# Where the last weights of a two-layer decoder wait, and in which order its first tiles are asked for

## The chip, the cores and the metric

The kernel runs on one core of one Trainium2 chip, in one launch. The metric is device time in microseconds (us), the median of several runs. Everything below comes from those times and from one profiled execution of the kernel before.

## What is computed

Two layers of a hybrid decoder over 1104 tokens (1024 of a prompt, 16 learned ones ahead of it, 64 of eight sampled sequences), width 1024, float32. Cut to what matters:

```python
def trunk_layer(x, pos, lw, states, front_pad, chunk, attend):
    m, new_states = hybrid_mixer(rmsnorm(x, lw['g_pre_mix']), pos, lw, states, front_pad, chunk, attend)
    x = x + rmsnorm(m, lw['g_post_mix'])
    gate, up = jnp.split(rmsnorm(x, lw['g_pre_ffn']) @ lw['w_ffn_in'], 2, axis=-1)
    x = x + rmsnorm((jax.nn.silu(gate) * up) @ lw['w_ffn_out'], lw['g_post_ffn'])
    return x, new_states
```

The mixer projects the normalized input (`w_in`), runs three token mixers on its columns (gated delta rule, a state space model, sliding-window attention with rotary positions) and projects back (`w_out`). The hidden width of the last block (SwiGLU) is 2816.

## The kernel before

**Arithmetic.** Each float32 operand of a large matrix product is split into two float16 parts, a rounded one (an ACT cast) and a residual (a VectorE operation), and a product takes three matmuls: high by high, high by low, low by high. For a weight this split is made on the chip, piece by piece: a piece of 128 x 1024 is loaded raw, cast, and its residual taken.

**Tiles.** Tokens stand in nine tiles of 128 (the last has 80), so `NT` is 9. The last projection of a layer (`w_ffn_out`) is done in seven half-size products, in Strassen's manner, instead of eight: `FSEQ` (line 35) gives their order 1, 2, 5, 6, 3, 7, 4. Their weights are blocks of `w_ffn_out` or sums and differences of blocks. Products 7 and 4, the last two, take a difference between a raw block and a running sum that is kept in `tcx`. Each product walks over 11 blocks of rows in six pieces (the last piece is half as long), and has four output tiles of 128 tokens, plus a fifth of 80 in four of the seven.

**Order.** There is no order written out by hand. `Plan` (from line 116) keeps a clock for each engine from rough costs, and `run` takes generators by rank: the first in rank order whose inputs are due by TensorE's planned time goes on by one step, and if none is due, the one due first. Small ranks come first: 0 for norms and chains, 2 for the sums of the hidden activations (`hid_sums`), 3 for the two `loader` generators, 9 for `dense`, which issues the large products. The framework beneath may then move an instruction ahead on its engine when its own simulation has it ready sooner; DMA issues on SP are moved in this way too.

**Slots.** `big` hands out 23 general slots (`NG`), counted by `live`: `hold` takes one, `free` gives one back, `room(n)` waits for n. Beside them stand two raw slots (`rawp`, counted in `wfree["raw"]`), three slots `w`, and three slots `w2` in the last block. The queue that `order_loads` fills sets the order of all weight loads: `loader` takes the next piece when a raw slot is free, issues its DMA, waits until it is that piece's turn to be split and until it has somewhere to go (`avail`), splits it, and gives the raw slot back. For products 7 and 4 the queue alternates between a piece of 7 and one of 4. Pieces of 7 go to `w2`; of product 4 the first five go to general slots, the last to `w2`. `dense` drops a piece when all output tiles of its group are done; the groups of a product are pieces 0, 1, 2, 3 and then 4 with 5.

**Norms.** `ffn_post` runs after the last projection, in two generators of rank 0: per tile it loads the residual stream, squares and sums on ACT, takes the reciprocal root on POOL (`rsqrt`), multiplies by the gain and adds on VectorE, and stores. In layer 0 it goes on with the norm that makes layer 1's input (`norm_t`): another square, POOL step and product, eight transposes on TensorE, and casts and residuals. It starts for four tiles after product 3, and for the other four after product 4.

**Start.** `norm0` loads and norms the tiles of x; `first_load` loads and splits the four pieces of the first weight. Four `norm0` generators are started among the first loads, so four tiles of x are asked for early, and each later one when a generator has finished a tile.

Of the kernel before, what the change touches and what calls it, by code (L numbers as in the profile page):

```python
# [8 lines left out]
F32 = mybir.dt.float32  # L9
# [30 lines left out]
def tsz(i):  # L40
    return 128 if i < 8 else 80
# [74 lines left out]
class Plan:  # L116
# [9 lines left out]
    def __init__(self):  # L126
        self.clk = dict.fromkeys("TVSGD", 0.0)
        self.wr = {}
        self.done = {}
        self.banks, self.start, self.acc = {}, {}, {}  # L130
        self.tasks = []
        self.last = 0.0

# [72 lines left out]
    def engine(self, eng, k):  # L206
        plan = self

        class E:
            def __getattr__(self, name):  # L210
                f = getattr(eng, name)

                def call(*a, **kw):
                    r = f(*a, **kw)  # L214
                    aps = [x for x in list(a) + [v for n, v in kw.items() if n not in ("out", "accum_out")]
                           if isinstance(x, bass.AP)]
                    out = kw.get("out")
                    if out is None:
                        out, aps = aps[0], aps[1:]
                    plan.note(k, name, out, aps, [kw["accum_out"]] if "accum_out" in kw else [],  # L220
                              kw.get("op") is ALU.pow)
                    return r

                return call

        return E()
# [55 lines left out]
def build(tc, A, depth=DEPTH):  # L282
    nc = tc.nc
    P = Plan()
    V, S, G, T, DQ = (P.engine(e, k) for e, k in ((nc.vector, "V"), (nc.scalar, "S"), (nc.gpsimd, "G"),
# [176 lines left out]
    def loader():  # L462
        while True:
            yield lambda: wfree["raw"] > 0 and took[0] < len(queue) and not seven[0]
            if wfree["raw"] == 0 or took[0] == len(queue) or seven[0]:
                continue
# [6 lines left out]
            if src is not None:  # L473
                wfree["raw"] -= 1
                raw = rawp.tile([128, 1024], F32, tag="raw", name="raw")[:, :n]
                dma(raw, src)
# [5 lines left out]
            def avail():  # L482
                if split[0] != my:
                    return False
                if where == "t":
                    return key[2] == 0 or ("ffn", key[1]) in done and (
                        wfree["w2"] > 0 if key[2] != 4 or key[3] == 5 else live[0] < NG)
# [14 lines left out]
            if where == "f":  # L502
                where = "w2" if wfree["w2"] else "w"
            elif where == "t":
                where = "g" if key[2] == 4 and key[3] < 5 else "w2"
            elif where != "w":
                where = "g"
# [18 lines left out]
            if src is not None:  # L526
                wfree["raw"] += 1
# [160 lines left out]
    def order_loads(L):  # L688
# [16 lines left out]
        for ns in ((1,), (2, 0), (5,), (6,), (3,), (7, 4)):  # L705
# [125 lines left out]
    def dense():  # L831
        for L in LY[:depth]:
# [234 lines left out]
            for n in FSEQ:  # L1067
                bk = [psd.tile([128, 512], F32, tag="d", name="pd") for _ in range(2)] + [PS("o") for _ in range(2)]
                for g in ((0,), (1,), (2,), (3,), (4, 5)):
# [63 lines left out]
    def norm0(L, it):  # L1133
        for i in it:
            C = tsz(i)
            yield room(1)
            hold()
            xt = big([128, D], F32, "xt")
            dma(xt[:C], A["x"][i * 128:i * 128 + C, :])
            yield None  # L1140
            yield (("gb0",),)
# [974 lines left out]
    P.add(0, norm0(L, it))  # L2116
    P.run()
    dma(c32, A["c32"])
    load_g(0, 0, L.gb0)
    for s in range(4):  # L2120
        P.add(-1, first_load(s))
        P.run()
        if s in (1, 2):
            P.add(0, norm0(L, it))
            P.run()
    P.add(0, norm0(L, it))
    P.add(3, loader())
    P.add(3, loader())
    P.add(0, when([("xn", 0, i) for i in range(NT)], free))
    mark(("gb0",))  # L2130
    P.add(9, dense())
    P.add(1, setup(L))
    for L in LY[:depth]:
# [10 lines left out]
        P.run(("swaend", l), ("gates", l), *((("zt", l, i), "st") for i in range(NT)))  # L2144
        sub.close()
# [40 lines left out]
        P.add(0, ffn_post(L, it))  # L2186
        P.add(0, ffn_post(L, it))
# [92 lines left out]
```

## Time and profile before

| | us |
|---|---|
| median of 3 runs | 2901.14 |
| lowest and highest | 2896.04 and 2902.44 |
| the profiled execution | 2895.58 |
| its span, first to last instruction | 2893.5 |
| TensorE busy / VectorE busy / ACT busy / POOL busy | 2743.2 / 1933.3 / 1288.4 / 813.1 |
| mean granted TensorE clock | 0.981 |

The profile names an instruction by its engine (PE is TensorE, PEld its weight loads, DVE is VectorE, POOL is GpSimd, SP issues the DMAs), by what it writes and reads (`wsp<-raw` is a split of a raw piece, `hsp<-hid` one of the hidden activations, `rqy<-ss` the reciprocal root of a norm, `m` and `xt` the output and the residual stream of a tile), and by its shape. All lines are line 214, the recorder through which every call goes. An idle time stands in brackets with what ended it. A busy share tells how full an engine is; TensorE's own time also depends on its granted clock, of which 1.0 is 2.4 GHz and 0.5 is 1.2 GHz.

### The profile page before, as it was taken

What the parts mean: (1) busy time and instruction counts of PE and PEld (TensorE: products, weight loads), DVE (VectorE), ACT (ScalarE), POOL (GpSimd) and SP (SyncE); (2) the same over time, 40 slices, a digit from 0 to 9 for tenths busy, and PEclk for the clock granted to TensorE, in tenths of its full rate; (3) what the DMA queues carried; (4) which work ended last, traced back from release to release, by engine and by line L of the source; (5) the groups of instructions that cost most, each with busy time, mean ns of one, the idle gap of its engine ahead of it and who ended that gap; (6) DMA issues with size and microseconds to landing.
All of it is one profiled execution on the core that took longest, in us unless ns stands there. A gap on an engine that the chain in (4) does not pass through costs nothing. (4 is left out here: it accounts for less than half of the span.)

```text
span 2893.5 us, 50019 instructions
## 1 busy us (share of the span) xinstructions
PE 2743.2 (95%) x19662; PEld 1909.5 (66%) x19662; DVE 1933.3 (67%) x3614; ACT 1288.4 (45%) x3015; POOL 813.1 (28%) x1124
## 2 busy tenths in 40 slices
PE   6999999999799999999899999999998999999997
PEld 3766677664588888744348676777646888886443
DVE  5557667655757676767865676666457666766776
ACT  5435456554423333433544455655543333334342
POOL 2204523313543333200260062223136233231011
PEclk8999999999899999999999999999999999999998
DMA  5011110132301111242431111001222111113333
GB/s 183 31 60 37 57 38 31 38 104 89 109 30 59 53 51 59 96 120 68 163 128 34 50 47 46 31 31 56 86 103 87 50 54 59 52 52 110 106 115 124
DMA packets 74092, 209.79 MB, mean 73 GB/s; under 512 B 13360, under 2 KB 24816, under 8 KB 73824
## 3 DMA queue, kind: packets, MB, share of 16 engines
q1 hardware_dynamic: 73856, 206.59, 21.8%
q8 instruction: 154, 2.52, 0.4%
q14 instruction: 82, 0.67, 0.1%
HBM read 175.49 MB, written 33.04 MB: 72 GB/s over the span
## 5 line engine op out<-in xcount | busy, mean ns | idle before, releaser
L214 PEld LDWEIGHTS <-wsp 128*128 128x128 f16 x10704 | 1044.1, 99 | 305.7 <-issue 12.9
L214 PE MATMUL pd<-xn,wsp 128*128 128x336 f16 (+3 forms) x4512 | 737.7, 311 | 3.4 <-DVE a L214 3.1
L214 DVE SCALAR_TENSOR_TENSOR wsp<-raw,wsp 128x512 f16<-128x512 f32 (+2 forms) x414 | 404.8, 986 | 196.3 <-ACT wsp L214 193.5
L214 ACT ACTIVATE wsp<-raw 128x512 f16<-128x512 f32 (+2 forms) x414 | 311.0, 763 | 393.5 <-DVE raw L214 145.9
L214 PEld LDWEIGHTS <-hsp 128*128 128x128 f16 x1848 | 182.1, 99 | 242.0 <-issue 30.2
L214 PE MATMUL pd<-wsp,hsp 128*128 128x512 f16 x924 | 232.6, 385 | 17.1 <-ACT wsp L214 11.8
L214 PE MATMUL ps_o<-wsp,hsp 128*128 128x512 f16 x924 | 230.7, 383 | 0.5 <-DVE m L214 0.5
L214 PE MATMUL pd<-wsp,mixed 128*128 128x512 f16 (+1 forms) x864 | 212.0, 384 | 5.8 <-DVE m L214 5.8
L214 POOL TENSOR_SCALAR rqy<-ss 128x1 f32<-128x1 f32 (+1 forms) x72 | 56.1, 779 | 551.1 <-ACT jk L214 407.6
L214 DVE SCALAR_TENSOR_TENSOR u<-R,lp_cw,u 128x512 f32<-128x512 f32 x216 | 180.0, 869 | 4.3 <-ACT u L214 3.4
L214 ACT ACTIVATE hsp<-hid 128x512 f16<-128x512 f32 x154 | 89.8, 620 | 180.4 <-PE ps_o L214 143.7
L214 PE MATMUL pd<-wsp,xn 128*128 128x512 f16 (+3 forms) x864 | 161.2, 338 | 6.0 <-ACT wsp L214 3.4
L214 PE MATMUL ps_o<-xn,wsp 128*128 128x256 f16 (+1 forms) x1296 | 165.1, 285 | 0.0
L214 POOL TENSOR_TENSOR raw<-raw 128x512 f32<-128x512 f32 x74 | 95.5, 1292 | 241.9 <-DVE raw L214 208.4
L214 PE MATMUL ps_inv<-xn,wsp 128*128 128x256 f16 (+1 forms) x1248 | 154.0, 281 | 0.8 <-DVE a L214 0.8
L214 POOL TENSOR_TENSOR U<-U,hid 128x256 f32<-128x256 f32 (+1 forms) x114 | 80.3, 733 | 239.3 <-ACT hid L214 239.3
L214 PEld LDWEIGHTS <-mixed 128*128 128x128 f16 (+1 forms) x864 | 84.4, 101 | 82.4 <-issue 11.3
L214 DVE TENSOR_TENSOR hsp<-hid,hsp 128x512 f16<-128x512 f32 x154 | 101.4, 684 | 43.3 <-ACT hsp L214 43.3
L214 PEld LDWEIGHTS <-xn 128*128 128x128 f16 (+1 forms) x864 | 87.4, 103 | 55.9 <-issue 10.7
L214 PE MATMUL ps_ch<-xn,wsp 128*128 128x296 f16 x456 | 109.2, 289 | 0.0
L214 PE MATMUL ps_tr<-xn,wsp 128*128 128x256 f16 x456 | 108.6, 273 | 0.0
L214 DVE TENSOR_TENSOR W<-ps_inv,c 128x512 f16<-128x512 f32 (+1 forms) x120 | 71.0, 595 | 46.3 <-PE ps_inv L214 45.4
(496 smaller groups left out, 4738.9 us busy)
## 6 DMA issues: line engine op xcount, KB each, us to landing
raw<-wfi SPq DMA_DIRECT2D x88, 512.0 KB, 3.5
raw<-wfo SPq DMA_DIRECT2D x70, 512.0 KB, 3.7
raw<-wf SPq DMA_DIRECT2D x44, 512.0 KB, 3.3
xd<-xt SPq DMA_DIRECT2D x24, 512.0 KB, 2.9
xt<-xd SPq DMA_DIRECT2D x24, 512.0 KB, 5.7
xt<-x SPq DMA_DIRECT2D x16, 512.0 KB, 6.1
raw<-wo SPq DMA_DIRECT2D x16, 512.0 KB, 3.4
tcx<-wfo SPq DMA_DIRECT2D x10, 512.0 KB, 3.7
```

Source lines behind the costliest of these rows:

```text
L214: r = f(*a, **kw)
```

## The change

Five things. Raw pieces of products 7 and 4 no longer use the two raw slots: each takes a general slot (tag `rawg`), which it gives back after its split; a loader may start on them even when no raw slot is free. All pieces of 7 now come ahead of those of 4 in the queue, all finished pieces of 4 go to `w2`, and product 4's last group is made of pieces 3, 4 and 5. There are three loaders instead of two. The two `ffn_post` generators have rank 4 instead of 0, behind `hid_sums` (2) and the loaders (3). At the start `load_x` asks for all nine tiles of x by itself: the first ahead of the constants, one more with each of the later pieces of the first weight, and the rest at once behind the fourth; three `norm0` generators then only compute. And until the attention of layer 0 has ended, every DMA issue is pinned behind the one before it on SP (`P.pin`), so that the framework no longer moves them.

```diff
--- before.py
+++ after.py
@@ -130,6 +130,7 @@
         self.banks, self.start, self.acc = {}, {}, {}
         self.tasks = []
         self.last = 0.0
+        self.pin = None
 
     @staticmethod
     def box(a):
@@ -212,6 +213,8 @@
 
                 def call(*a, **kw):
                     r = f(*a, **kw)
+                    if k == "D" and plan.pin is not None:
+                        plan.pin(r)
                     aps = [x for x in list(a) + [v for n, v in kw.items() if n not in ("out", "accum_out")]
                            if isinstance(x, bass.AP)]
                     out = kw.get("out")
@@ -282,6 +285,7 @@
 def build(tc, A, depth=DEPTH):
     nc = tc.nc
     P = Plan()
+    P.pin = tc.keep_in_program_order
     V, S, G, T, DQ = (P.engine(e, k) for e, k in ((nc.vector, "V"), (nc.scalar, "S"), (nc.gpsimd, "G"),
                                                  (nc.tensor, "T"), (nc.sync, "D")))
     dma = DQ.dma_start
@@ -461,8 +465,11 @@
 
     def loader():
         while True:
-            yield lambda: wfree["raw"] > 0 and took[0] < len(queue) and not seven[0]
-            if wfree["raw"] == 0 or took[0] == len(queue) or seven[0]:
+            def more():
+                k = took[0] < len(queue) and queue[took[0]][0]
+                return k and (wfree["raw"] > 0 or k[0] == "w2" and k[2] in (7, 4)) and not seven[0]
+            yield more
+            if not more():
                 continue
             my = took[0]
             took[0] += 1
@@ -470,7 +477,13 @@
             if where == "s":
                 yield from load7(my, key, src)
                 continue
-            if src is not None:
+            spare = key[0] == "w2" and key[2] in (7, 4)
+            if spare:
+                yield room(1)
+                hold()
+                raw = big([128, 1024], F32, "rawg")[:, :n]
+                dma(raw, src)
+            elif src is not None:
                 wfree["raw"] -= 1
                 raw = rawp.tile([128, 1024], F32, tag="raw", name="raw")[:, :n]
                 dma(raw, src)
@@ -483,8 +496,7 @@
                 if split[0] != my:
                     return False
                 if where == "t":
-                    return key[2] == 0 or ("ffn", key[1]) in done and (
-                        wfree["w2"] > 0 if key[2] != 4 or key[3] == 5 else live[0] < NG)
+                    return key[2] == 0 or ("ffn", key[1]) in done and wfree["w2"] > 0
                 if where == "f":
                     return ("ffn", key[1]) in done and wfree["w2"] + wfree["w"] > 0
                 if where == "w":
@@ -502,7 +514,7 @@
             if where == "f":
                 where = "w2" if wfree["w2"] else "w"
             elif where == "t":
-                where = "g" if key[2] == 4 and key[3] < 5 else "w2"
+                where = "w2"
             elif where != "w":
                 where = "g"
             if where == "g":
@@ -523,7 +535,9 @@
             stt(w[:, 1, :n], x, WS, w[:, 0, :n], MUL, SUB)
             if key[0] == "w2" and key[2] == 5:
                 V.tensor_tensor(x, raw, x, op=SUB)
-            if src is not None:
+            if spare:
+                free()
+            elif src is not None:
                 wfree["raw"] += 1
             if key[0] == "w2" and key[2:] == (4, 5):
                 mark(("tcend", key[1]))
@@ -702,7 +716,7 @@
                     want(("wi", l, c, z), src[z], 1024, "f")
             else:
                 want(("wi", l, c), src, 1024, "s")
-        for ns in ((1,), (2, 0), (5,), (6,), (3,), (7, 4)):
+        for ns in ((1,), (2, 0), (5,), (6,), (3,), (7,), (4,)):
             for n, s in [x for s in range(7) for x in ((ns[0], s), (ns[-1], s - 1))[:len(ns)] if 0 <= x[1] < 6]:
                 want(("w2", l, n, s), None if n == 6 else wfo(l, *FW[n], s), (2 if s < 5 else 1) * 512, "t")
 
@@ -1066,7 +1080,7 @@
                    for i in range(8)}
             for n in FSEQ:
                 bk = [psd.tile([128, 512], F32, tag="d", name="pd") for _ in range(2)] + [PS("o") for _ in range(2)]
-                for g in ((0,), (1,), (2,), (3,), (4, 5)):
+                for g in ((0,), (1,), (2,), (3,), (4, 5)) if n != 4 else ((0,), (1,), (2,), (3, 4, 5)):
                     yield tuple((x, l, n, q) for x in ("w2", "S2") for q in g)
                     ks = range(2 * g[0], min(2 * g[-1] + 2, NF // 2))
                     for t in (0, 2, 1, 3, 4):
@@ -1132,13 +1146,7 @@
 
     def norm0(L, it):
         for i in it:
-            C = tsz(i)
-            yield room(1)
-            hold()
-            xt = big([128, D], F32, "xt")
-            dma(xt[:C], A["x"][i * 128:i * 128 + C, :])
-            yield None
-            yield (("gb0",),)
+            xt, C = L.x0[i], tsz(i)
             yield from norm_t(xt, C, i, L.gb0, L.xn, xt, "n")
             free()
             mark(("xn", 0, i))
@@ -2113,21 +2121,27 @@
     L = LY[0]
     it = iter(range(NT))
     L.gb0 = big([128, D], F32, "gb0")
-    P.add(0, norm0(L, it))
-    P.run()
+    L.x0 = []
+
+    def load_x(n):
+        for i in range(len(L.x0), n):
+            hold()
+            L.x0.append(big([128, D], F32, "xt"))
+            dma(L.x0[i][:tsz(i)], A["x"][i * 128:i * 128 + tsz(i), :])
+
+    load_x(1)
     dma(c32, A["c32"])
     load_g(0, 0, L.gb0)
-    for s in range(4):
+    for s, n in enumerate((1, 2, 3, 4)):
         P.add(-1, first_load(s))
         P.run()
-        if s in (1, 2):
-            P.add(0, norm0(L, it))
-            P.run()
-    P.add(0, norm0(L, it))
-    P.add(3, loader())
-    P.add(3, loader())
+        load_x(n)
+    load_x(NT)
+    for _ in range(3):
+        P.add(0, norm0(L, it))
+    for _ in range(3):
+        P.add(3, loader())
     P.add(0, when([("xn", 0, i) for i in range(NT)], free))
-    mark(("gb0",))
     P.add(9, dense())
     P.add(1, setup(L))
     for L in LY[:depth]:
@@ -2142,6 +2156,7 @@
         P.add(0, swa_out(L))
         P.add(1, gates(L))
         P.run(("swaend", l), ("gates", l), *((("zt", l, i), "st") for i in range(NT)))
+        P.pin = None
         sub.close()
         sub = ExitStack()
         L.ssp = pool("ssm", 1, stack=sub)
@@ -2183,8 +2198,8 @@
         if not L.last:
             P.add(1, setup(LY[l + 1]))
         it = iter((0, 1, 2, 3, 8, 4, 5, 6, 7))
-        P.add(0, ffn_post(L, it))
-        P.add(0, ffn_post(L, it))
+        P.add(4, ffn_post(L, it))
+        P.add(4, ffn_post(L, it))
         P.run(("dense", l), *(x for i in range(NT) for x in (("fp", l, i), (("x", l, i), "st"))))
         wfree["w2"] = 0
         free(2 if L.last else 3)
```

## Rows read from the trace of the kernel before

**Rows 1.** Page, part 1: busy us, share of the span, instructions.

```profile
PE 2743.2 (95%) x19662; PEld 1909.5 (66%) x19662; DVE 1933.3 (67%) x3614; ACT 1288.4 (45%) x3015; POOL 813.1 (28%) x1124
```

**Rows 2.** Windows: length, busy us (instructions) by engine, PE clock, DMA share, GB/s.

```profile
0.00:75.00 75.00, 48.79 (x249) 27.85 (x249) 37.45 (x66) 37.01 (x85) 23.17 (x45) 0.86 0.52 177
...
1385.00:1463.00 78.00, 67.68 (x310) 30.53 (x309) 69.81 (x83) 41.34 (x67) 17.58 (x19) 0.96 0.54 177
1463.00:1500.00 37.00, 31.98 (x161) 16.15 (x160) 26.11 (x41) 17.49 (x34) 27.56 (x35) 0.95 0.36 110
2810.00:2882.00 72.00, 62.60 (x268) 27.06 (x266) 53.61 (x64) 26.08 (x40) 13.78 (x10) 0.93 0.39 129
2882.00:2894.00 12.00, 0.23 (x2) 0.00 (x0) 7.81 (x8) 2.30 (x4) 3.57 (x5) 0.70 0.43 175
```

**Rows 3.** Windows of 25 us: the same point of layer 0 and layer 1.

```profile
300.00:325.00 25.00, 20.54 (x150) 15.19 (x150) 22.14 (x48) 11.67 (x35) 14.52 (x19) 0.97 0.15 47
...
1725.00:1750.00 25.00, 20.52 (x144) 14.93 (x143) 20.81 (x45) 10.33 (x31) 14.05 (x19) 0.93 0.14 42
```

**Rows 4.** Timeline of layer 1's product 7: start, length, engine, operation, count.

```profile
2810.63 1.46 PE L214 MATMUL pd<-wsp,hsp 128*128 128x512 f16 x6
...
2811.93 1.46 PE L214 MATMUL ps_o<-wsp,hsp 128*128 128x512 f16 x6
```

**Rows 5.** Timeline of the start; in brackets idle time and what ended it.

```profile
8.48 1.11 PE L214 MATMUL ps_tr<-c,xt 128*128 128x128 f32 x4 [8.48 <-DVE xt L214]
...
14.53 0.43 SPq L214 DMA_DIRECT2D raw<-wtA  x1
...
17.85 8.13 SPq L214 DMA_DIRECT2D xt<-x  x5
...
23.37 1.06 ACT L214 ACTIVATE wsp<-raw 128x1024 f16<-128x1024 f32 x1
...
45.12 1.06 ACT L214 ACTIVATE xn<-xt 80x1024 f16<-80x1024 f32 x1 [1.05 <-POOL rqy L214]
```

**Rows 6.** Windows of 5 us, columns as in rows 2.

```profile
10.00:15.00 5.00, 4.56 (x15) 1.34 (x14) 3.19 (x5) 1.91 (x3) 0.00 (x0) 1.00 1.09 287
35.00:40.00 5.00, 4.71 (x15) 2.58 (x15) 1.89 (x2) 3.92 (x9) 4.63 (x7) 0.50 0.28 110
2815.00:2820.00 5.00, 5.00 (x25) 2.29 (x24) 5.00 (x6) 2.16 (x5) 5.00 (x1) 1.00 0.59 166
```

**Rows 7.** Groups by shape, 1385 to 1463 us: busy us, mean ns | idle before.

```profile
L214 DVE SCALAR_TENSOR_TENSOR m<-xt,rqy,gb 128x1024 f32<-128x1024 f32 x4 | 5.1, 1279 | 1.3 <-POOL rqy L214 1.3
...
L214 PE MATMUL ps_tr<-c,m 128*128 128x128 f32 x16 | 2.5, 282 | 1.4 <-DVE m L214 1.4
```

**Rows 8.** Groups by shape, 2810 to 2882 us, columns as in rows 7.

```profile
L214 DVE TENSOR_TENSOR hsp<-hid,hsp 128x512 f16<-128x512 f32 x20 | 13.3, 684 | 7.8 <-ACT hsp L214 7.8
...
L214 DVE SCALAR_TENSOR_TENSOR wsp<-raw,wsp 128x1024 f16<-128x1024 f32 x9 | 11.0, 1221 | 1.6 <-ACT wsp L214 1.6
...
L214 ACT ACTIVATE wsp<-raw 128x1024 f16<-128x1024 f32 x8 | 8.4, 1053 | 12.8 <-DVE raw L214 12.8
...
L214 DVE SCALAR_TENSOR_TENSOR xt<-m,rqy,xt 128x1024 f32<-128x1024 f32 x5 | 6.4, 1279 | 0.8 <-POOL rqy L214 0.7
...
L214 DVE TENSOR_TENSOR raw<-raw,tcx 128x1024 f32<-128x1024 f32 x4 | 4.9, 1216 | 0.0
```

**Rows 9.** Timeline of products 7 and 4 in layer 1.

```profile
2815.86 3.21 SPq L214 DMA_DIRECT2D raw<-wfo  x2
...
2826.52 0.59 PE L214 MATMUL pd<-wsp,hsp 128*128 128x512 f16 x1 [5.37 <-ACT wsp L214]
...
2842.17 0.38 PE L214 MATMUL pd<-wsp,hsp 128*128 128x512 f16 x1 [2.24 <-ACT wsp L214]
```

**Rows 10.** Timeline of the end.

```profile
2887.34 2.47 DVE L214 SCALAR_TENSOR_TENSOR xt<-m,rqy,xt 128x1024 f32<-128x1024 f32 x2
```

**Rows 11.** POOL's norm step, 2800 us to the end: ns least/median/most, first and last start.

```profile
L214 POOL TENSOR_SCALAR rqy<-ss x9: 190/1221/7667, 2805.6 to 2885.3; 128x1 f32<-128x1 f32 x8, 80x1 f32<-80x1 f32 x1
```

## The prediction, written before the result was known

> **What bounds the kernel now.** I read the page's busy times first: TensorE is busy 2743.2 us, 95% of the span, VectorE 1933.3 [rows 1]. So TensorE sets the end, and time can be won only where it is idle or at its lower clock. Next comes the busy time by stage: nearly every window is full of TensorE; three places are not, and the change touches all three [rows 2]. The start: 48.79 us busy of the first 75.00, granted clock 0.86. The seam between the layers (last products of layer 0, then the first projection of layer 1): 10.3 us idle of 78.00, then 5.0 of 37.00. The last products of layer 1: 9.4 us idle of 72.00 at clock 0.93, and after the last matmul (0.23 us into the last window, so at 2882.23) 11 us with no TensorE.
>
> How much the start loses is read by comparing the layers. The window 300 to 325 us has 20.54 us of TensorE, the window 1725 to 1750 has 20.52 [rows 3]: the same point of the layer. Layer 0 comes to it 300 us after the span's start; layer 1 comes to it 262 us after 1463, where its first projection begins (the cut of rows 2). So the start costs 38 us more than a start with everything at hand.
>
> For the last two products (7 and 4) I need their floor. Six matmuls start at 2810.63 and the next six at 2811.93 [rows 4], so one takes 0.216 us; the two products have 2 x 11 x 4 x 3 = 264 of them: 57.0 us. In layer 1 they take 72, so 15.0 are lost: 9.4 idle, and clock 0.93 means 14% of 72, about 10 us, at the 1.2 GHz level, where half the progress is lost: 5.0. The sum, 14.4, agrees.
>
> **The change, part by part. Start.** Nothing is removed; transfers are moved. Before, the fourth piece of the first weight was asked for at 14.53 us, behind constants, the next weight and copies of caches; five tiles of x followed from 17.85, and that issue took 8.13 us, each waiting for earlier transfers [rows 5]. Now SP's queue keeps program order: x0, constants, gain, four weight pieces with x1 to x3 between, then x4 to x8. Up to the fourth piece and x3 that is, by their shapes, 0.52 MB x 9 + 0.3 = 5.0 MB. At the 287 GB/s of the window 10 to 15 us [rows 6] this needs 17 us, and some 2 more to land: the fourth piece is there at 17 to 19 us and all of x (2.4 MB more) by 27, where before the fourth split ran at 23.37 and the square of the last tile at 45.12 [rows 5]. TensorE still cannot start before 8.48 [rows 5], and to finish the first tile it needs the fourth piece. A tile costs it 24 x 0.216 = 5.2 and eight transposes at 2.5 / 16 each [rows 7], together 6.4 us, more than VectorE's 2.7 for its norm (1.28 + 2 x 0.68 [rows 7, 8]), so once x is there TensorE sets the pace. Loss after, as an estimate: 12 idle (18 less one tile's 6.4), up to 4 before the second tile, 3 at the low clock, 6 for waits inside the attention steps, together 25 against 38. I take **-12**; bounds -3 (the tiles were late by engine queues, not by transfers) and -17 (no gap and almost no waits). What is moved behind x (rotary tables, second weight, cache copies, convolution weights: some 4 MB, 14 us) lands near 41 us. SP's pinned order could hold a load behind a store that waits for its engine; the cover is that from 75 us on TensorE works from weights already split. If it is gone, a first rotary step waits a few us on POOL, while TensorE has nine tiles of projection to do: 0, bound +3.
>
> **Last products, layer 1.** Before, two raw slots alternate between a piece of 7 and one of 4, and a slot comes back only after VectorE's residual, which stands behind norm work. So the third piece of 7 is asked for at 2815.86, and TensorE stops 5.37 us at 2826.52, then 2.24 at 2842.17 [rows 9]. The change gives each raw piece a general slot, has three in flight, takes all of 7 ahead of 4, and lets splits go before norms. Number and duration of the splits stay: 1.22 for the difference, 1.22 for the residual, 0.68 for each half-width operation [rows 8]. VectorE's whole work in the window is 53.61 us [rows 2], below the 57.0 floor, so it has room if the order is right. What the change takes away: product 4 loses its five general slots for finished weights and shares three with product 7. Such a slot comes free two groups (10.4 us) before its next piece is needed; difference, cast and residual need 1.22 + 1.05 + 1.22 = 3.5 [rows 8]. Its last group, of three pieces, needs the last of them right after the second group, but twelve matmuls (2.6 us) come ahead of it. For this and for the change from 7 to 4 I leave 4 of the 14.4: **-10.5**; bounds -14 and -4.
>
> **Tail.** The last group of product 4 has five blocks instead of three, so its four output tiles finish 15 x 0.216 = 3.24 us apart, not 1.94. One tile's eviction, gain and addition need 0.68 + 1.22 + 1.28 = 3.2 us of VectorE [rows 8], so no queue builds up. Today two additions run until 2889.8 [rows 10], 7.6 us after the last matmul; one tile's chain without a queue (0.68, then 1.05, POOL's two steps, 1.28 and the hops) ends about 5 us after it. **-2.5**; bounds -4 and 0 (five norms now rank lower and may land here, but the last 13 us of matmuls ask little else of VectorE).
>
> **Seam.** Here norms also make layer 1's input, so a tile costs VectorE 1.22 + 1.28 + 1.28 + 2 x 0.68 = 5.1 us [rows 7, 8]. In the 115 us of both windows VectorE is busy 95.9 and TensorE 99.7 [rows 2], the latter about 95 at full clock. So no more than 19 us can be had, and VectorE becomes the bound as soon as TensorE's waits go. Splits put first push norms into the projection; that alone does not lose, since a tile costs TensorE 6.4 there against 5.1. With VectorE nine tenths busy the 115 become 106.6: I take **-7**; bounds -14 and 0.
>
> Elsewhere the third loader finds no raw slot, except where a piece needs none: 0, bounds 3 either way, since the planner's order shifts.
>
> Sum: -12 - 10.5 - 2.5 - 7 = -32. The profiled execution took 2895.6 us in all (its span 2893.5); 2895.6 - 32 = 2863.6. The median of the runs shown, 2901.1, is 5.5 higher, and I carry that over: **2869**.
>
> **A rule against it.** POOL's small step of a norm takes 0.19 us at best in the last stretch and 7.67 at worst [rows 11]; in the window 2815 to 2820, inside that worst one, POOL holds one instruction for 5.00 us while VectorE is busy 5.00 of 5.00 [rows 6]. The Trainium skill ("SBUF — State Buffer", section "Who interferes with whom") has VectorE with two SBUF inputs and GpSimd reading SBUF exclude each other, the later one blocking fully. By that rule, with which the row agrees, splits packed ahead of norms keep POOL out longer.
>
> **The rivals.** First, x was not the limit: the last tile's load was issued by 26 us, its square ran at 45.12 [rows 5]. Against it: transfers still moved 110 GB/s at 35 to 40 us [rows 6]. Then the start gives 3, not 12: 2878. Second, the ranking does nothing, because the planner takes a norm when it comes ready and a split only when VectorE is due to be free; only the earlier loads work, and half of the products' and the seam's gain stays away: 2869 + 5 + 3.5, about 2878. Third, norms starve: POOL's step finds no gap, as in its 7.67 us, the gains and additions of five tiles (5 x 2.5 = 12.5 us) run after the last matmul, and the seam gives nothing: 2869 + 12.5 + 7, about 2888. Against it stands VectorE's room in the last group. Fourth, slower: product 4 with three slots waits at each piece. It decides when more than 10.4 - 3.5 = 6.9 us of other VectorE work stands ahead of a split; two norms of layer 0 make 10.2, so it can. Each wait costs what the second of layer 1 did, 2.24 idle and about 1.9 of low clock; five pieces in two layers make 41 us. Against these stand the start's 12, the tail's 2.5 and product 7's first wait (5.4 and 3 of clock in layer 1, perhaps 5 in layer 0): +13, so 2914. Fifth, the change doesn't do what it says: engine orders replace each wait by another: 2901.
>
> **How the numbers follow.** Forecast 0.55; rivals one to five 0.12, 0.10, 0.10, 0.08, 0.05. The first three are faster too, by more than 0.2% (5.8 us, about what a measurement of this kernel can tell from no change). So faster 0.87, same 0.05, slower 0.08. The range: down to 2869 - 17 = 2852, where each part comes near its better bound; up to 2889, which takes in the first three rivals. Left out are the last two rivals (0.13) and about 0.07 beside.
>
> **What the profile would show.** Start: the fourth piece split before 20 us, the last tile's square before 32, TensorE busy over 58 of the first 75 us; the step is wrong under 52. Products in layer 1: about 61 us for 7 and 4 and no wait above 2 us inside 7; wrong if a wait for a cast or residual stands at each piece of 4. Seam: VectorE over nine tenths busy until the last norm; wrong if the projection still waits for norms. Tail: under 9.5 us from the last matmul to the end. The whole is wrong if the stage 75 to 1385 us, which I leave alone, moves by more than 3 us.

## The result, and where the time went

| | us |
|---|---|
| kernel after, median of 4 runs | 2858.06 (2854.41 to 2860.39) |
| kernel before, beside it, median of 4 runs | 2898.91 (2896.04 to 2902.44) |
| ratio, with its 95% interval | 0.9857 (0.9839 to 0.9875) |
| profiled execution after, its span | 2859.83, 2858.0 |

The change saves 40.85 us, 1.4%. The two profiled executions differ by 35.5 us in span; the other 5 are the choice of execution: that of before lies just below the runs shown, that of after near the top of its own.

Both kernels run the same stages in the same order, so the span can be cut where a stage's first matmul starts or a store begins:

| stage (us) | before | after | difference | forecast |
|---|---|---|---|---|
| start, to the store of layer 0's convolution states | 588.8 | 577.5 | -11.3 | -12 |
| from there to layer 0's product 7 | 796.9 | 798.4 | +1.5 | 0 |
| layer 0, products 7 and 4 | 77.2 | 69.5 | -7.7 | seam: |
| first stage of layer 1, to its store | 549.6 | 544.9 | -4.7 | -7 together |
| from there to layer 1's product 7 | 798.1 | 798.4 | +0.3 | 0 |
| layer 1, products 7 and 4 | 71.6 | 58.9 | -12.7 | -10.5 |
| last matmul to the end | 11.3 | 10.4 | -0.9 | -2.5 |
| sum | 2893.5 | 2858.0 | -35.5 | -32 |

Page of after, part 1 (busy us, share of the span, instructions), and windows of after that answer to [rows 1, 2] (length, busy us (instructions) by engine, PE clock, DMA share, GB/s):

```profile
PE 2730.1 (96%) x19662; PEld 1907.6 (67%) x19662; DVE 1938.0 (68%) x3614; ACT 1287.5 (45%) x3015; POOL 820.8 (29%) x1124
```

```profile
0.00:75.00 75.00, 56.42 (x326) 34.32 (x327) 49.02 (x83) 43.80 (x103) 28.18 (x50) 0.91 0.56 185
...
1376.00:1445.50 69.50, 63.42 (x291) 29.56 (x290) 61.88 (x74) 37.27 (x59) 23.71 (x20) 0.95 0.44 140
1445.50:1482.50 37.00, 37.00 (x198) 19.65 (x197) 26.86 (x35) 15.63 (x30) 31.20 (x38) 1.00 0.36 118
2788.70:2847.60 58.90, 57.44 (x265) 25.54 (x263) 51.41 (x62) 25.11 (x38) 14.98 (x9) 1.00 0.45 145
2847.60:2858.00 10.40, 0.00 (x0) 0.00 (x0) 6.07 (x6) 1.65 (x4) 3.56 (x4) 0.68 0.38 151
```

The recorder's line is 215 now, for 214. The number of instructions on each of these engines is as before, and VectorE's time is 4.7 us above it. TensorE's busy time falls by 13.1 us with the same matmuls (its mean granted clock rises from 0.981 to 0.984), its idle time by 22.4. Layer 1's products are now full but for 1.46 us, at granted clock 1.00, where 0.93 stood. In layer 1's first projection TensorE is busy 37.00 of 37.00, where it was 31.98, while VectorE has only 26.86: it is not what bounds there.

The waits of TensorE inside layer 1's products (engine and tile that waited, for whom: us in total, times, longest) have one line left, where [rows 9] showed waits of 5.37 and 2.24 for casts:

```profile
PE pd L215 <- DVE hsp L215: 1.5, 1, 1.5
```

SP's timeline of the start and ACT's, which answer to [rows 5] (start, length, operation):

```profile
2.58 0.44 SPq L215 DMA_DIRECT2D lp_cw<-cw  x1
...
4.01 0.45 SPq L215 DMA_DIRECT2D raw<-wtB  x1
4.50 0.43 SPq L215 DMA_DIRECT2D raw<-wtA  x1
...
8.79 0.43 SPq L215 DMA_DIRECT2D xt<-x  x1
9.27 0.43 SPq L215 DMA_DIRECT2D raw<-wtA  x1
...
10.21 0.84 SPq L215 DMA_DIRECT2D k_s<-ck  x1
...
11.53 0.43 SPq L215 DMA_DIRECT2D raw<-wtA  x1
12.01 0.68 SPq L215 DMA_DIRECT2D v_s<-cv  x1
12.74 6.29 SPq L215 DMA_DIRECT2D xt<-x  x6
```

```profile
20.29 1.04 ACT L215 ACTIVATE wsp<-raw 128x1024 f16<-128x1024 f32 x1
...
36.13 1.05 ACT L215 ACTIVATE xn<-xt 80x1024 f16<-80x1024 f32 x1
```

The pin does not do what the diff seems to say. Convolution constants, pieces of the second weight and copies of caches still stand ahead of x1 and of the later weight pieces. In program order the constants come behind x8. Read from the program, the pin hangs each DMA on the last instruction traced on SP, whatever that is, and ahead of the constants that is not x8's DMA, so from there the chain floats as a whole; no run shows this reason by itself. What is traced after `P.pin = None` (layer 1's constants, for one) is not held at all. Still, the last six tiles of x are asked for from 12.74 us, where it was five from 17.85, and the fourth weight piece at 11.53 instead of 14.53.

### The profile page after: what moved, and what is told of

Its sections match the earlier page's. It is cut to its first block, busy times and chain, and to the rows that moved or that the text cites. A ratio compares the mean times of both kernels' runs of the same rounds, so it can differ in the third digit from the quotient of the medians.

```text
span 2858.0 us, 50012 instructions
## 1 busy us (share of the span) xinstructions
PE 2730.1 (96%) x19662; PEld 1907.6 (67%) x19662; DVE 1938.0 (68%) x3614; ACT 1287.5 (45%) x3015; POOL 820.8 (29%) x1124
## 5 line engine op out<-in xcount | busy, mean ns | idle before, releaser
L215 PEld LDWEIGHTS <-wsp 128*128 128x128 f16 x10704 | 1044.4, 99 | 306.3 <-issue 14.6
L215 DVE SCALAR_TENSOR_TENSOR wsp<-raw,wsp 128x512 f16<-128x512 f32 (+2 forms) x390 | 377.4, 977 | 184.1 <-ACT wsp L215 181.3
L215 ACT ACTIVATE wsp<-raw 128x512 f16<-128x512 f32 (+2 forms) x390 | 287.4, 749 | 367.3 <-DVE raw L215 106.5
L215 PE MATMUL pd<-wsp,hsp 128*128 128x512 f16 x924 | 224.5, 381 | 3.8 <-DVE hsp L215 1.9
L215 PE MATMUL ps_o<-wsp,hsp 128*128 128x512 f16 x924 | 222.5, 379 | 0.0
L215 POOL TENSOR_SCALAR rqy<-ss 128x1 f32<-128x1 f32 (+1 forms) x72 | 65.5, 910 | 528.1 <-ACT jk L215 390.9
L215 DVE SCALAR_TENSOR_TENSOR u<-R,lp_cw,u 128x512 f32<-128x512 f32 x216 | 180.3, 870 | 11.3 <-ACT u L215 10.3
```

## The experiments

All are edits of the kernel after. The table gives the stages as above, and the ratio to the kernel before, measured beside each. The first two rows are the kernels before and after. Stages are in us, each from one profiled execution.

| kernel | start | L0 7+4 | L1 first | L1 7+4 | tail | median us | ratio (95%) |
|---|---|---|---|---|---|---|---|
| before | 588.8 | 77.2 | 549.6 | 71.6 | 11.3 | 2898.9 | |
| after | 577.5 | 69.5 | 544.9 | 58.9 | 10.4 | 2858.1 | 0.9857 (0.9839 to 0.9875) |
| after again | 577.1 | 68.1 | 545.2 | 59.0 | 10.4 | 2856.0 | 0.9846 (0.9827 to 0.9866) |
| start alone | 575.1 | 77.6 | 552.9 | 70.8 | 11.6 | 2883.3 | 0.9954 (0.9941 to 0.9966) |
| last products alone | 591.2 | 68.1 | 548.1 | 58.9 | 10.4 | 2873.1 | 0.9911 (0.9897 to 0.9924) |
| no pin | 578.6 | 67.9 | 544.9 | 58.9 | 10.4 | 2863.1 | 0.9879 (0.9865 to 0.9892) |
| pin that holds | 575.6 | 68.2 | 547.9 | 58.9 | 10.5 | 2859.3 | 0.9867 (0.9851 to 0.9882) |
| norms at rank 0 | 574.7 | 68.6 | 551.3 | 58.9 | 10.4 | 2861.5 | 0.9867 (0.9852 to 0.9882) |
| two loaders | 574.8 | 68.0 | 548.8 | 58.8 | 10.5 | 2857.8 | 0.9853 (0.9836 to 0.9869) |
| raw slots | 572.9 | 66.8 | 558.0 | 64.6 | 9.7 | 2871.5 | 0.9904 (0.9889 to 0.9918) |
| small last group | 576.6 | 71.4 | 561.8 | 59.0 | 11.6 | 2877.1 | 0.9921 (0.9906 to 0.9936) |
| small group, layer 1 | 574.8 | 68.4 | 544.7 | 58.9 | 11.2 | 2857.2 | 0.9852 (0.9838 to 0.9867) |
| three norm generators | 575.1 | 66.9 | 553.4 | 59.6 | 10.5 | 2865.0 | 0.9888 (0.9872 to 0.9905) |
| the same, pin that holds | 575.5 | 67.0 | 554.2 | 59.6 | 10.5 | 2866.7 | 0.9891 (0.9876 to 0.9906) |

### The unchanged kernel again

> The kernel after once more, unchanged: how far do the stages of one program differ between two executions? Six kernels with the same start had the store of layer 0's convolution states at 572.9 to 577.5. Theory (that spread comes from the planned order, which each edit shifts): here it is at 577.5 within 0.3, and layer 1's first stage (end of product 4 to that layer's store) is 544.9 within 0.5. Rival (it is the execution): the first differs by 1 to 3, the second by over 1.

The store stands at 577.1, the first stage of layer 1 takes 545.2, each within 0.4 us of the first execution (products 7 and 4 of layer 0 differ by 1.4). Two executions say little about a spread, but other kernels below say more. Up to the store, the traces of eight more executions (this one, start alone, norms at rank 0, two loaders, raw slots, both kernels with small groups, three norm generators) hold the same operations on the same tiles in the same order as after's, on every engine. Their stores begin at 572.9 to 577.1, with after's nine executions from 572.9 to 577.5, 575.4 on the mean. So that spread is not the planned order, as the theory had it: the order is one, and the execution makes the difference. In the same way last products alone, no pin, pin that holds and small group in layer 1 have after's order between the two stores: their first stage of layer 1 takes 544.7 to 548.1 us, and layer 0's products 7 and 4 take 67.9 to 69.5. In the start a difference of less than 5 us, and in that stage one of less than 3.5, is not put down to a kernel here.

Inside the start this execution was later: the fourth piece split at 22.50 us, the last tile's square at 38.16, 2 us behind the first execution. Still at 249 us, after's TensorE was 4.0 us ahead (its 1600th matmul at 249.1, here at 253.1). It lost most of that with TensorE as busy but at a lower granted clock, as the windows of after and of this execution show:

```profile
300.00:400.00 100.00, 96.33 (x736) 68.29 (x735) 60.24 (x120) 50.28 (x116) 22.95 (x40) 0.95 0.13 44
```

```profile
300.00:400.00 100.00, 96.29 (x749) 69.09 (x747) 61.61 (x127) 51.40 (x118) 22.90 (x41) 0.97 0.13 44
```

Between 200 and 300 us the clock was 0.98 against 1.00. So the equal stores are a matter of the two executions.

### The start, alone and taken away

Start alone (the conditions under which a loader starts and splits a piece also go back to those of before):

```diff
...
-            spare = key[0] == "w2" and key[2] in (7, 4)
+            spare = False
...
-                where = "w2"
+                where = "g" if key[2] == 4 and key[3] < 5 else "w2"
...
-        for ns in ((1,), (2, 0), (5,), (6,), (3,), (7,), (4,)):
+        for ns in ((1,), (2, 0), (5,), (6,), (3,), (7, 4)):
...
-                for g in ((0,), (1,), (2,), (3,), (4, 5)) if n != 4 else ((0,), (1,), (2,), (3, 4, 5)):
+                for g in ((0,), (1,), (2,), (3,), (4, 5)):
...
-    for _ in range(3):
+    for _ in range(2):
         P.add(3, loader())
...
-        P.add(4, ffn_post(L, it))
+        P.add(0, ffn_post(L, it))
```

Last products alone (`norm0` loads its own tile again):

```diff
-    P.pin = tc.keep_in_program_order
...
-    load_x(1)
+    P.add(0, norm0(L, it))
+    P.run()
...
-        load_x(n)
-    load_x(NT)
+        if s in (1, 2):
+            P.add(0, norm0(L, it))
+            P.run()
```

> The kernel after with everything of the last products undone (two raw slots, 7 and 4 alternating, two loaders, norms at rank 0): only the start of the change is left. Theory: the start is worth 11 us by itself, so the store of layer 0's convolution states begins near 577.5 us as in the kernel after (588.8 before), and the time is about 2888, 0.996 of before; both stages of last products read as before (39 and 38 us in layer 0, 43 and 28.6 in layer 1). Rival (the start's gain in the kernel after comes in part from a third loader, which works in that stage too): the store begins above 580 us and the time is 2893 or more.

> The kernel after with the start of before (tiles of x asked for as a norm generator comes free, no order on SP's issues). Theory: the start is lost again and nothing else, so the store of layer 0's convolution states begins at 588 to 590 us, the rest keeps its differences against before (layer 0's product 7 -8, layer 1's first projection -4.7, layer 1's product 7 -12.8), and the time is about 2870, 0.990 of before. The gains add up: this kernel's and the start's together give what the change gives. Rival (the third loader alone disturbs the start or the stages between): the sum of both is over 4 us from the change's.

The start alone is worth 0.46% (13.3 us), the last products alone 0.89% (25.8); the sum, 39, is what the change gives, 41, within the intervals. In the traces the old start has its store at 588.8 and 591.2, the new one at 572.9 to 578.6 in all the others. The theory holds. In the start kernel layer 1's first stage is 3.3 longer than before; between the two stores it has the order of before on every engine, so this too is a spread of executions.

### Which part of the start's edit works

```diff
-    P.pin = tc.keep_in_program_order
```

> The kernel after without the order on SP's issues; all nine tiles of x are still asked for at once. Theory (asking early is what counts, since in the kernel after the order is broken by the convolution constants anyway and second weight pieces and cache copies float ahead of x): the fourth piece of the first weight and the last tiles of x come at most 2 us later, the store of layer 0's convolution states begins at 577 to 580 us, time as after. Rival (the order carries the gain, as the prediction put it): the store begins above 583 us and half of the start's gain is gone.

Pin that holds: everything through the last tile of x in one chain, every later DMA behind that tile.

```diff
-    P.pin = tc.keep_in_program_order
+    ahead = []
+    def behind(r):
+        if ahead:
+            tc.add_manual_dep(r.ins, ahead[-1].ins.name,
+                              mybir.DependencyInfo(mybir.DependencyClass.NoSync, mybir.DependencyReason.DATA),
+                              reason="behind")
+    def chain(r):
+        behind(r)
+        ahead.append(r)
+    P.pin = chain
...
     load_x(NT)
+    P.pin = behind
...
-        P.pin = None
```

> The kernel after with an order on SP that holds: everything through the last tile of x in one chain, and every other transfer behind it (in the kernel after two second-weight pieces, two sets of convolution constants and two cache copies stand ahead of the last tiles of x). Theory, by the prediction's own step: the fourth piece is split by 19 us instead of 20.29, the square of the last tile runs by 30 instead of 36.13, and the store of layer 0's convolution states begins 2 to 5 us earlier than 577.5; time 2854. Rival (TensorE's own work per tile sets the pace once the first tiles are there): the transfers come earlier but the store begins within 1 us of 577.5. A loss would come from the second weight and the rotary tables, which now come last: then a wait on a rotary step stands in the trace between 40 and 75 us.

Without the pin the store is at 578.6, 3.2 above the mean of after's order, and the time can't be told from after's; the fourth piece is split 2.7 us later than in after, where at most 2 were expected. So the gain, but for a few us at most, comes from asking for all tiles at once, not from the order. With the order that holds, the transfers come as the prediction had said, as ACT's timeline of that kernel shows:

```profile
18.16 1.05 ACT L215 ACTIVATE wsp<-raw 128x1024 f16<-128x1024 f32 x1
...
31.08 1.05 ACT L215 ACTIVATE xn<-xt 80x1024 f16<-80x1024 f32 x1
```

and the store is at 575.6 (575.5 in the second kernel with this start). That is 2.0 before after's, at the near edge of what the theory expected, but it is where the nine executions with after's order have it on the mean, 575.4. What followed from the rival holds: five microseconds on the last tile buy nothing that can be seen at the store. Its reason, TensorE's own work, is not what the trace shows in the windows 100 to 150 us, of after and of this kernel:

```profile
100.00:150.00 50.00, 50.00 (x458) 41.26 (x457) 24.61 (x75) 18.84 (x73) 6.34 (x12) 1.00 0.18 56
```

```profile
100.00:150.00 50.00, 47.42 (x416) 38.58 (x414) 22.38 (x64) 18.40 (x71) 5.64 (x9) 0.97 0.21 68
```

TensorE, which by 100 us has some 520 matmuls behind it against some 500 in after, stands 2.6 us here, waiting for VectorE, and its granted clock is 0.97 (the second kernel with this start does the same, the other eight executions with after's order are full here, as after is). So a part of the lead at least is given back in waits for VectorE. The loss feared for the tables is not in the trace: no rotary step on POOL waits for a transfer.

### Which part of the last products' edit works

Norms at rank 0, and, in another kernel, two loaders:

```diff
-        P.add(4, ffn_post(L, it))
+        P.add(0, ffn_post(L, it))
```

```diff
-    for _ in range(3):
+    for _ in range(2):
         P.add(3, loader())
```

> The kernel after with the two norm generators of the last block back at rank 0, ahead of the sums of the hidden activations and of the loaders. Theory (splits ahead of norms is a part of the gain of its own): with norms first, product 7 waits for a split again while the norms of the four tiles of product 3 run; product 7 takes 34 to 38 us in layer 1 instead of 30.2 and 34 to 38 in layer 0 instead of 31.1, and the time is 5 to 12 above after. Rival (the second one of the prediction: the planner takes a norm when it comes ready and a split only when VectorE is due to be free, so ranks decide nothing): both products stay within 1 us and the time within 0.1%.

> The kernel after with two loaders instead of three. A piece is needed every 10.4 us and its load lands some 3 us after it is asked for. Theory (two in flight are enough once raw pieces don't wait for a slot): product 7 within 1 us of 31.1 and 30.2, product 4 without waits, time as after. Rival (three in flight are needed because a loader stands in the queue until its split is done): product 7 takes 2 to 5 us more in each layer, the time is 3 to 8 above.

Layer 1's products take 58.9 and 58.8 us, as with the whole change. So in these products the rank decides nothing beside the new order and slots, as the prediction's second rival had it, and a third loader isn't needed (a piece lasts 24 matmuls of 0.216 us, so one is needed every 5.2 us, not every 10.4 as was expected). At the seam, the rank kernel's first stage of layer 1 is 6.4 longer, over the spread of one order, and TensorE's order there is another; in time it can't be told from after.

Raw slots: the pieces of 7 and 4 are loaded into the two raw slots again, in the new order, and a loader starts on one only when a raw slot is free.

```diff
...
-            spare = key[0] == "w2" and key[2] in (7, 4)
+            spare = False
```

> The kernel after with the raw pieces of products 7 and 4 back in the two raw slots; order of the pieces, ranks, loaders and groups as after. Theory, by the prediction's steps (a raw slot comes back only after the residual, and product 7's first pieces were asked for too late): product 7 takes 3 to 8 us more than 31.1 and 30.2 in each layer, with one wait for a cast or a residual of a split; the time is 6 to 14 above after. Rival (the order of the pieces and the ranks alone carry the gain, since splits no longer stand behind norms and so the slots come back in time): product 7 within 1.5 us, time within 3.

The cost was as the theory said, its place was not. Product 7 takes 31.0 us in layer 1, 0.8 more; product 4 takes 33.6 instead of 28.7. TensorE's waits in these two products:

```profile
PE pd L215 <- ACT wsp L215: 2.7, 1, 2.7
PE pd L215 <- DVE hsp L215: 2.1, 2, 1.8
```

and why, from SP's timelines, of this kernel and of after:

```profile
2817.84 23.73 SPq L215 DMA_DIRECT2D raw<-wfo  x5
```

```profile
2801.50 4.54 SPq L215 DMA_DIRECT2D rawg<-wfo  x3
```

With raw slots the last five pieces are asked for between 23 and 47 us after product 7 begins (2794.6); with general slots all have been asked for after 17 (2788.7). The slots give the 5.7 us from 64.6 to 58.9. The 7.0 from 71.6 to 64.6 are left to the rest of the edit; as ranks, loaders and the last group change nothing here in the kernels beside it (58.8 to 59.0), they are put down to the order of the pieces, with all finished pieces of 4 in `w2`, but no kernel has that alone. Its first stage of layer 1 takes 13 us longer than after's, layer 0's products 2.7 less; with raw slots the order on the engines there is another, and what of it costs the 13 was not settled.

### The last group and the seam

```diff
-                for g in ((0,), (1,), (2,), (3,), (4, 5)) if n != 4 else ((0,), (1,), (2,), (3, 4, 5)):
+                for g in ((0,), (1,), (2,), (3,), (4, 5)):
```

> The kernel after with product 4's last group of two pieces (1.5 pieces of work) instead of three, so that the last four tiles finish 1.94 us apart instead of 3.24. Theory, by the prediction: the tail from the last matmul to the end is 1 to 2.5 us longer than 10.4, product 4 stays at 28.6; the time is 1 to 2.5 above after, which the rounds may not resolve but the profile does. Rival (the tail is set by one tile's chain after its eviction, whatever stands before it): the tail is within 0.5 us of 10.4.

The tail is 1.2 longer, as expected, but the kernel loses 19 us, nearly all at the seam. Its first projection of layer 1, TensorE's timeline, and below it VectorE's:

```profile
1451.58 16.35 PE L215 MATMUL pd<-wsp,xn 128*128 128x512 f16 x75
1467.77 0.44 PE L215 MATMUL ps_tr<-c,m 80*128 80x80 f32 x4
```

```profile
1445.64 1.28 DVE L215 SCALAR_TENSOR_TENSOR m<-xt,rqy,gb 80x1024 f32<-80x1024 f32 x1
...
1457.48 1.61 DVE L215 SCALAR_TENSOR_TENSOR xt<-m,rqy,xt 128x1024 f32<-128x1024 f32 x1
1468.72 0.49 DVE L215 TENSOR_TENSOR xn<-ps_tr,xn 128x320 f16<-128x320 f32 x1 [9.63 <-ACT xn L215]
```

The tile of 80 tokens is ready for its transposes at 1447, but they stand behind 75 matmuls of the projection, until 1467.77. VectorE's next instruction needs them, so VectorE idles 9.63 us, the norms of the last tiles slip, and then TensorE waits for those (10.4 us in all until 1505). In the kernel after the same transposes stand behind 27 matmuls:

```profile
1446.76 5.99 PE L215 MATMUL pd<-wsp,xn 128*128 128x512 f16 x27
1452.58 0.44 PE L215 MATMUL ps_tr<-c,m 80*128 80x80 f32 x4
```

The large group in layer 0 only:

```diff
-                for g in ((0,), (1,), (2,), (3,), (4, 5)) if n != 4 else ((0,), (1,), (2,), (3, 4, 5)):
+                for g in ((0,), (1,), (2,), (3,), (4, 5)) if n != 4 or L.last else ((0,), (1,), (2,), (3, 4, 5)):
```

> The kernel after with the large last group of product 4 in layer 0 only; layer 1 has the two groups of before. Theory (in the run with the small groups in both layers, the 17 us were lost at the seam of the layers by the order in which transposes of norms and the first projection stand on TensorE, and layer 1's group is worth only its tail): layer 1's first stage is 545 to 548 as in the kernel after, the tail is 11.4 to 11.8, the time 0 to 4 above after. Rival (the 17 us come from elsewhere, for instance from layer 1's own plan): the stage stays above 555 and the time above 2870.

The seam is whole again (544.7), the tail 0.8 longer where at least 1.0 was expected, the time as after. Between the two stores this kernel has after's order on every engine. So the 17 us belong to layer 0's group, and what it changed is the order; how much of them the transposes alone cost is read from the trace, not from a kernel of its own.

A third norm generator, alone and with the pin that holds:

```diff
-        P.add(4, ffn_post(L, it))
-        P.add(4, ffn_post(L, it))
+        for _ in range(3):
+            P.add(4, ffn_post(L, it))
```

> The kernel after with three norm generators in the last block instead of two, so that a third tile's residual stream can be asked for and its norm begun before the first of the four last tiles is done. Theory (each tile's chain is a chain over four engines whose steps wait for one another, and what limits the tail is the chain of the last tile: eviction 1.7 us after the last matmul because the gain of the tile before stands ahead of it on VectorE, then 5.2 us to its addition): a third generator doesn't shorten that, the tail stays within 0.5 us of 10.4, and the seam of the layers moves by at most 3 us either way with the planned order. Rival (the two generators are the limit of the tail and of the seam): the tail falls below 9.5, the first projection of layer 1 is 3 us shorter or more, the time 3 to 8 below after.

> Both together: the order on SP that holds until the last tile of x, and three norm generators. Theory: the sum of the two alone, each within 3 us of after, so 2853 to 2860 and not told from after by the rounds. Rival (both limits are real and add): below 2852.

The tail stays at 10.5: generators are not its limit. But the first stage of layer 1 takes 8.5 us more (layer 0's products 2.6 less), and the ratio is 0.003 worse; the theory's bound of 3 us for the seam was wrong. With both edits the kernel is no better than with the generators alone, so what was expected of the pair fell as well. No kernel here is faster than the kernel after by more than the intervals.

## Why the prediction held, and where it did not

The forecast was 2869 us, the result is 2858, inside the range and in the direction given. Against its own profile the sum of -32 meets -35.5.

**Start**: -11.3 against -12. The size was met by the luck of one execution: over all kernels with the new start the store is 10 to 18 us earlier than with the old, and after's is the latest of nine executions with its order; their mean, 575.4, against 590.0 for the two with the order of before, is -14.6, still within the bounds. The mechanism, that tiles were late by their requests, is shown by the two kernels that keep one half, and the first rival (x not the limit) falls. Three finer statements failed. "SP's queue keeps program order" was read from the diff: it does not, by the timeline above. So the fourth split came at 20.29, not before 20, the last square at 36.13, not before 32, and TensorE was busy 56.42, not over 58. And the step that made the gain follow from the time of the last tile was too simple: with the order that holds all three marks are met (18.16, 31.08, 59.12), and the gain is no larger.

**Last products of layer 1**: -12.7 against -10.5. Of the 14.4 us that were lost above the floor of 57.0, I left 4 for the last group and for the change from 7 to 4; 1.9 are left. The waits that went are the ones named, and product 4 with three slots, the fourth rival, did not wait: it takes 28.7 us, of 28.5. The marks set for it are met: about 61 us, and no wait above 2. Wrong was the part given to ranks. The second rival's premise is true here (ranks decide nothing in these products); its price, half of the gain, is not, since the rest of the edit gives it all, the slots 5.7 of it.

**Seam**: -12.4 against -7, within its bounds of -14 and 0. Product 7 of layer 0 gave 8.2 of it (39.2 to 31.0), product 4 nothing (38.0 and 38.4), the stage behind them 4.7. The step that failed is the limit: "VectorE becomes the bound". VectorE was busy 0.89 of layer 0's products and 0.73 of the window behind them, and the mark "over nine tenths" was missed. What the kernel with the small group shows in its place is how transposes and projection are ordered on TensorE, with VectorE in turn waiting behind them. In kernels that share the new start and most of the last products, this stage took from 544.7 to 561.8. An estimate from busy times can't see that; the size of this term was partly luck, and of the 4.7 up to 3.4 can be the execution. Why the planned order turns with these edits was not settled.

**Tail**: -0.9 against -2.5, and 10.4 us where under 9.5 was the mark. VectorE's timeline of after, and POOL's:

```profile
2848.15 1.22 DVE L215 TENSOR_TENSOR m<-m,gb 128x1024 f32<-128x1024 f32 x1
...
2849.28 0.68 DVE L215 SCALAR_TENSOR_TENSOR m<-ps_o,m 128x512 f32<-128x512 f32 x1
...
2851.29 1.22 DVE L215 TENSOR_TENSOR m<-m,gb 128x1024 f32<-128x1024 f32 x1
2851.32 1.23 POOL L215 TENSOR_SCALAR rqy<-ss 128x1 f32<-128x1 f32 x1 [1.27 <-ACT jk L215]
...
2853.22 1.28 DVE L215 SCALAR_TENSOR_TENSOR xt<-m,rqy,xt 128x1024 f32<-128x1024 f32 x1 [0.71 <-POOL rqy L215]
```

The last matmul ends at 2847.6, the last addition at 2854.5: 6.9 us, where the step had "about 5". Two terms were left out. The eviction starts 1.7 after the last matmul, because the gain of the tile before stands ahead of it; and POOL's step takes 1.23 instead of 0.19, exactly beside the tile's own gain on VectorE. The queue of two additions at the end [rows 10] is gone, as foreseen.

**The lock.** POOL's norm steps are held as long as before [rows 11]. In product 7 of layer 1, POOL's timeline of after:

```profile
2790.73 8.39 POOL L215 TENSOR_SCALAR rqy<-ss 128x1 f32<-128x1 f32 x1 [1.68 <-ACT jk L215]
```

VectorE's nine operations from 2790.32 to 2799.07 follow one another without a gap, all with both inputs in SBUF, and the step ends at 2799.12. The longest hold is in the kernel with three norm generators, in layer 0's product 7; POOL's timeline, and VectorE's at its end:

```profile
1375.92 21.51 POOL L215 TENSOR_SCALAR rqy<-ss 128x1 f32<-128x1 f32 x1 [2.57 <-DVE xt L215]
```

```profile
1396.17 1.22 DVE L215 SCALAR_TENSOR_TENSOR wsp<-rawg,wsp 128x1024 f16<-128x1024 f32 x1
1397.30 1.28 DVE L215 SCALAR_TENSOR_TENSOR m<-pd,m 128x512 f32<-128x512 f32 x2
```

There VectorE works without a gap on operations with two SBUF inputs, and the step ends at 1397.43, just after VectorE has begun an eviction, which reads one input from PSUM. So a gap is not needed, an operation of the other kind is enough; in after a step beside an eviction (at 2788.22) takes 0.19. The rule of the Trainium skill ("SBUF — State Buffer", section "Who interferes with whom"), that VectorE with two SBUF inputs and a GpSimd operation that reads SBUF shut each other out, agrees with these rows and with the 1.23 of the tail; but the hold lasts over the whole run of such operations, not over one. Whether the 21.51 us make the seam of that kernel longer was not separated. The third rival, norms that starve into the end, did not come: a norm held in product 7 has all of product 4 to recover. The change does not shorten the lock; the one wait of TensorE that is left in layer 1's products, 1.5 us, is for a sum of hidden activations (`hsp`).

**Elsewhere**: the two long stages between moved by +1.5 and +0.3, within the bound of 3.

## What to carry to other kernels

Where weights are loaded a piece at a time, look at when each raw piece is asked for, and what must come free first: here the request, not the transfer, nor its rank in the plan, was the wait. Read the real order of a queue in the trace before counting on a pin. Where two stages meet on in-order engines, judge an edit by the stage behind it too: a smaller last group cost 1.2 us at its own place and 17 us in the next layer. And before a few microseconds are put down to an edit, compare the order of operations on each engine: with one order, the same stage here ended up to 4.6 us apart.

## What was not expected of the chip

Nine executions with one order of operations end the start at 572.9 to 577.5, and a lead of 4.0 us was lost between 249 us and the store, where the granted clock was lower. The small POOL step, 0.19 us beside an eviction from PSUM, takes 1.23 where it starts beside one gain multiplication of VectorE, and 8.39 or 21.51 where VectorE runs operations with two SBUF inputs without a gap.
